# A hybrid RWKV-7 and forgetting-attention block: attention's logits tied to bulk steps, merge's first half in other banks, two gates moved

## The chip, the cores and the metric

The kernel is one program on one core of a Trainium2 chip. Its time is the device time in microseconds of one execution. TensorE (PE) does the matmuls and transposes, VectorE (DVE) and ScalarE (ACT) the elementwise work, GpSimd (POOL) some of it, and SyncE (SP) issues most DMAs. Each engine works through its own list of instructions in order. The order of these lists is fixed when the program is built.

## The reference

One block on x of 1024 tokens by 1024 channels, float32:

- h = rmsnorm(x) and u = h @ w_in, with 6,280 columns: for RWKV (r, k, v, two low-rank inputs, a gate), for attention (q, k, v, a gate, forget logits), and two gates g_a, g_b of 1,024 columns each.
- RWKV-7, 8 heads of 64: a token shift, then a scan over the tokens with a 64 x 64 state for each head, a norm for each head, a bonus term, times silu(gate).
- Forgetting attention, 8 heads of 64: q and k normed, logits q k / 8 plus the difference of cumulated log forget gates, causal softmax, times v, times silu(gate).
- merged = sigmoid(g_a) * (y_a @ w_out_a) + sigmoid(g_b) * (y_b @ w_out_b); then x + merged @ w_out and a last rmsnorm.

## The kernel before

Every projection is done in split precision: operands are kept as a high and a low part (`wH`, `wL`, `hTH`, `hTL`), and each k of the contraction takes three matmuls: high by high, high by low, low by high. The helper `laid` (L313) notes the third of them, so the list `laid_` has one entry for each such step, in the order in which the code emits them. A gate has 16 steps with 512 columns, a projection of v (two pairs of heads at once) 64 with 264 or 256, a projection of q and k for one pair 64 with 256.

The stages:

1. x is normed and transposed into `hTH` and `hTL`; the low-rank inputs and r, k, v of RWKV are projected.
2. RWKV runs in four units (pair of channel blocks p, half of the sequence n), here called units 0 to 3 = (0,0), (0,1), (1,0), (1,1). `prep` builds a unit's chunk matrices. Its matmuls `psc` (L587) come in two groups, and the second (e = 1) is the list `late_sc`. Behind it come masks on DVE, products on POOL, a bounce through DRAM and a triangular inverse by elimination on DVE (L663, L667), another bounce, transposes on DVE into `TW` (L679), and the small matmuls `pw` (L687) and `pz` (L698). Then `chain` walks through the unit's eight chunks, a serial chain of small matmuls and DVE and ACT work; `norm_out` ends the unit.
3. Attention runs over four pairs of heads. `project_qk` and `norm_qk` make q and k of a pair; `norm_qk` copies part of q to other partitions by DMA (QA<-QA, L988). `attend` goes over 8 blocks, four groups i of 256 queries by two heads h, with 2(i+1) parts of work in each: logits `sc` (L1024), a DVE pass (L1031), exp on ACT, transposes `pt`, products with V into `po`.
4. `merge` computes y_a @ w_out_a (`side` with key a: 16 tiles `pma`, 64 steps of 512 columns) and then y_b @ w_out_b (`pmb`). Its input `ya` takes the place of `hTL`, `m` that of `hTH`, and `yb` lies where attention's pool `fpa` lay, which holds V first of all. `parts` loads a piece of y through one of four ring slots and splits it on ACT (L1090) and DVE (L1091). The ring is used in fixed order; the pieces of `yb` are loaded between the columns c = 2 to 5 of the first half. Each `pma` tile is emptied by one DVE operation (L1124) with a gate piece `g`, loaded from `gab` through the same ring (L1118).
5. The last projection with w_out, the norm and the store.

What sets the order: every instruction has a priority, its place in the code. `order(LATER)` and `bulky()` put work far back, `order(-LATER)` far ahead. A planner walks a simulated time, and on each engine takes the instruction with the best priority whose operands are ready; this gives the fixed lists. Attention and `chain` are far ahead, and the "bulk" (gates, projections, merge) fills what they leave. The 24 gates are handed out by `fill`: RFILL[i] in the bulk of RWKV unit i; FPRE[p] before and FFILL[p] behind the projections of the next pair's q and k in `bulk_fox(p)`. Attention's pair 1 also has V of pairs 2 and 3 at the end of its bulk.

`not_before` adds an edge of program order without a semaphore: the named instructions come behind the given entry of `laid_` in PE's list. Before, it holds back `pw` of each unit, by PLACE; the call for `late_sc` is there but finds no name.

Bulk tiles go round PSUM banks by `bulk_tags`: RTAGS in RWKV, FTAGS (pj, pj, aux: three banks) in attention, TTAGS (seven) from merge on.

Of the kernel before, what the change touches and what calls it, by code (L numbers as in the profile page):

```python
# [53 lines left out]
PLACE = {  # L54
    "pw0_0": 179, "pw0_1": 294, "pw1_0": 398, "pw1_1": 502,
}
PACE = 0.3
# [19 lines left out]
RFILL = [5, 5, 3, 3]  # L77
FPRE = [1, 0, 0, 2]
FFILL = [1, 2, 2, 0]
# [15 lines left out]
def kernel(  # L95
# [215 lines left out]
    laid_ = []  # L311

    def laid(ins):  # L313
        laid_.append(ins.ins)

    def not_before(first, name):

        if name not in PLACE:
            return
        for ins in first:  # L320
            tc.add_manual_dep(
                ins, laid_[PLACE[name]].name,
                mybir.DependencyInfo(mybir.DependencyClass.NoSync, mybir.DependencyReason.DATA),
                reason="not_before",
            )
# [508 lines left out]
    def project_v(cb):  # L834
# [25 lines left out]
        for b in range(8):  # L860
# [3 lines left out]
            for k in range(KD):  # L864
                wH, wL = parts[k // KH]
                kk = k % KH
                nc.tensor.matmul(o, hTH[:, k, bs], wH[:, kk, :], start=(k == 0), stop=False)
                nc.tensor.matmul(o, hTH[:, k, bs], wL[:, kk, :], start=False, stop=False)
                laid(nc.tensor.matmul(o, hTL[:, k, bs], wH[:, kk, :], start=False, stop=(k == KD - 1)))
# [40 lines left out]
    def project_qk(p):  # L910
# [17 lines left out]
        for n in range(2):  # L928
            xt = fpa[0].tile([P, 4, QB], F32, tag="xn", name=f"xn{p}_{n}", bufs=2)
            rs = fpa[0].tile([P, 3, 16], F32, tag="rs", name=f"rs{p}_{n}", bufs=2)  # L930
            for b in range(4):
                bs = slice((4 * n + b) * P, (4 * n + b + 1) * P)
                ps = ps_pj(f"pf{p}_{n}_{b}")[:, :QB]
                for k in range(KD):
                    wH, wL = parts_[k // KH]
                    kk = k % KH
                    nc.tensor.matmul(ps, hTH[:, k, bs], wH[:, kk, :], start=(k == 0), stop=False)  # L937
                    nc.tensor.matmul(ps, hTH[:, k, bs], wL[:, kk, :], start=False, stop=False)  # L938
                    laid(nc.tensor.matmul(ps, hTL[:, k, bs], wH[:, kk, :], start=False, stop=(k == KD - 1)))  # L939
# [52 lines left out]
    sc_tags = SCTAGS  # L992

    def attend(p, KA, QA, qlo, cb):
        for i in range(4):
# [10 lines left out]
            for h, q in ((0, A), (1, B)):  # L1006
# [3 lines left out]
                for e in range(2):  # L1010
# [6 lines left out]
                    for g in range(ng):  # L1017
# [6 lines left out]
                        nc.tensor.matmul(sc[:, :mw], QA[:, h, qs], KA[:, h, ms], start=True, stop=False)  # L1024
# [74 lines left out]
    def merge():  # L1099
# [9 lines left out]
        with tc.tile_pool(name="yp", bufs=1, side="right", reuse_waits="tile") as yp:  # L1109
# [27 lines left out]
            for c in range(KD):  # L1137
                side(w_out_a, ya, 0, "a", c, then_a)
                if YB <= c < YB + 4:
                    for n in range(2):  # L1140
                        parts(c + 4 - YB, n, yb[:, 0], yb[:, 1])
            for c in range(KD):
# [52 lines left out]
    for p in range(4):  # L1195
        if not ATTFIRST:
            nxt = bulk_fox(p, None)
        with order(-LATER):
# [7 lines left out]
    bulk_tags[:] = TTAGS  # L1206
# [67 lines left out]
```

## Time and profile before

| | us |
|---|---|
| median of 3 runs (lowest to highest) | 1134.89 (1133.62 to 1138.43) |
| the profiled execution | 1135.76 |
| its span, first to last instruction | 1133.9 |
| mean granted clock of TensorE | 0.968 |
| DVE busy | 709.2 (63%) |
| ACT busy | 459.9 (41%) |
| POOL busy | 317.0 (28%) |

The span is cut into stages by what PE does: before 110 the input, the low-rank part and the first projections; RWKV's units up to about 597; attention's pairs, with borders at about 672, 748 and 860; merge from 944 to 1036; then the last projection. Times in the rows are microseconds from the span's start. A busy share counts an engine's records; matmuls overlap in them, so the pace of PE is read from the number of matmuls in a stretch. PEclk is the clock granted to TensorE, as a share of 2.4 GHz; it has the two levels 1.00 and 0.50. A value in brackets behind an instruction is the idle time of its engine before it and what ended that.

### The profile page before, as it was taken

To read this page: it belongs to the slowest core of one execution; us is meant where nothing else is said; L and a number is where in the kernel's file an instruction comes from. 1 tells how busy PE (TensorE), PEld (TensorE's weight loads), DVE (VectorE), ACT (ScalarE), POOL (GpSimd) and SP (SyncE) were. 2 spreads that over 40 slices of the span, in tenths; PEclk is the share of its full clock that TensorE was granted. 3 is DMA by queue.
4 is the path that set the end of the run, shared out by engine and by line. 5 is a ranking of instruction groups with operands and counts; after the bars stand their busy time and mean duration, and the time that the engine had idled before them with its cause. 6 is when DMAs were issued, how large, how long until landed. Compare 5 with 4: busy or idle time off the path is not lost. (4 is left out here: it accounts for less than half of the span.)

```text
span 1133.9 us, 18405 instructions
## 1 busy us (share of the span) xinstructions
PE 1052.9 (93%) x6591; PEld 871.7 (77%) x6591; DVE 709.2 (63%) x1855; ACT 459.9 (41%) x969; POOL 317.0 (28%) x467
## 2 busy tenths in 40 slices
PE   4989999999899999997998989979997999999997
PEld 3867777777677777777887877968896887887885
DVE  7414776699648883796678858652736823475145
ACT  6534323534243314431546636443544623223122
POOL 4420522252213421231113223222132222244400
PEclk9999999999989899998999989989998999999999
DMA  6256444144422433222024213232223126645133
GB/s 214 59 172 216 123 103 121 40 119 134 113 74 76 127 103 99 62 82 66 20 77 125 85 49 83 85 88 80 92 59 89 55 77 188 217 134 178 64 102 121
DMA packets 126684, 118.21 MB, mean 104 GB/s; under 512 B 33489, under 2 KB 91970, under 8 KB 126594
## 3 DMA queue, kind: packets, MB, share of 16 engines
q1 hardware_dynamic: 114304, 94.99, 29.1%
q10 hardware_dynamic: 11714, 21.52, 5.1%
q8 instruction: 52, 0.85, 0.3%
q0 software_dynamic: 576, 0.54, 0.2%
q14 instruction: 38, 0.31, 0.1%
HBM read 79.23 MB, written 35.68 MB: 101 GB/s over the span
## 5 line engine op out<-in xcount | busy, mean ns | idle before, releaser
L331 PE MATMUL ps_gg<-hTH,wH_gg 128*128 128x512 f32 x384 | 160.0, 417 | 0.8 <-DVE ql L982 0.6
L332 PE MATMUL ps_gg<-hTL,wH_gg 128*128 128x512 f32 x384 | 160.2, 417 | 0.0
L333 PE MATMUL ps_gg<-hTH,wL_gg 128*128 128x512 f32 x384 | 159.1, 414 | 0.0
L210 POOL TENSOR_TENSOR wL_gg<-w_gg,wH_gg 128x256 fp32r<-128x256 f32 x96 | 71.3, 774 | 194.2 <-ACT wH_gg L207 192.6
L331 PEld LDWEIGHTS ps_gg<-hTH,wH_gg 128*128 128x128 f32 x384 | 74.8, 195 | 15.5 <-issue 2.0
L333 PEld LDWEIGHTS ps_gg<-hTH,wL_gg 128*128 128x128 f32 x384 | 74.5, 194 | 13.9
L332 PEld LDWEIGHTS ps_gg<-hTL,wH_gg 128*128 128x128 f32 x384 | 74.6, 194 | 13.5
L938 PE MATMUL pf<-wqkL,hTH 128*128 128x256 f32 x256 | 73.7, 288 | 0.0
L939 PE MATMUL pf<-wqkH,hTL 128*128 128x256 f32 x256 | 73.7, 288 | 0.0
L937 PE MATMUL pf<-wqkH,hTH 128*128 128x256 f32 x256 | 73.5, 287 | 0.0
L396 ACT ACTIVATE gt<-ps_gg 128x512 f32<-128x512 f32 x40 | 23.9, 597 | 86.3 <-PE ps_gg L333 75.9
L1035 ACT ACTIVATE pr<-pr,mm 128x128 f32<-128x128 f32 (+3 forms) x64 | 49.9, 779 | 21.7 <-DVE mm L1031 19.4
L736 ACT ACTIVATE xw<-state,WC 64x64 f32<-64x64 f32 x112 | 38.7, 346 | 44.5 <-DVE state L756 37.3
L667 DVE TENSOR_TENSOR lt<-lt,etmp 64x30 f32<-64x30 f32 (+14 forms) x120 | 52.2, 435 | 3.7
L1228 PE MATMUL pz<-wo,mH 128*128 128x512 f32 (+1 forms) x136 | 52.4, 385 | 0.8 <-POOL wo L1097 0.8
L663 DVE TENSOR_TENSOR etmp<-lt 64x30 f32<-64x30 f32 (+14 forms) x120 | 47.7, 397 | 7.5 <-issue 4.0
L1227 PE MATMUL pz<-wo,mH 128*128 128x512 f32 (+1 forms) x136 | 51.8, 381 | 0.0
L1229 PE MATMUL pz<-wo,mL 128*128 128x512 f32 (+1 forms) x136 | 51.6, 379 | 0.0
L937 PEld LDWEIGHTS pf<-wqkH,hTH 128*128 128x128 f32 x256 | 49.2, 192 | 0.0
L938 PEld LDWEIGHTS pf<-wqkL,hTH 128*128 128x128 f32 x256 | 49.1, 192 | 0.0
L939 PEld LDWEIGHTS pf<-wqkH,hTL 128*128 128x128 f32 x256 | 49.0, 191 | 0.1
L1024 PE MATMUL sc<-KA,QA 128*128 128x384 f32 (+4 forms) x96 | 36.7, 390 | 12.0 <-DMA QA<-QA 11.9
(332 smaller groups left out, 2832.5 us busy)
## 6 DMA issues: line engine op xcount, KB each, us to landing
w_gg<-in_w_in_dram SPq DMA_DIRECT2D x24, 512.0 KB, 3.8
gab<-gt ACTq DMA_DIRECT2D x48, 256.0 KB, 2.0
ring<-gab SPq DMA_DIRECT2D x32, 256.0 KB, 3.1
xt<-in_x_dram SPq DMA_DIRECT2D x8, 512.0 KB, 6.1
wqk<-in_w_in_dram SPq DMA_DIRECT2D x16, 256.0 KB, 2.9
cb<-cumd SPq DMA_DIRECT2D x8, 512.0 KB, 4.1
ring<-yab SPq DMA_DIRECT2D x16, 256.0 KB, 3.7
ring<-in_w_out_dram SPq DMA_DIRECT2D x16, 256.0 KB, 3.1
```

The lines of the kernel that those rows point to most:

```text
L210: nc.gpsimd.tensor_sub(wL[:, k], w[:, k], wH[:, k])
L331: nc.tensor.matmul(ps, wH[:, k, :], rH[:, k, ts_], start=(k == 0), stop=False)
L332: nc.tensor.matmul(ps, wH[:, k, :], rL[:, k, ts_], start=False, stop=False)
L333: laid(nc.tensor.matmul(ps, wL[:, k, :], rH[:, k, ts_], start=False, stop=(k == nk - 1)))
L667: nc.vector.tensor_add(lt3[:, :s, s + 1 :], lt3[:, :s, s + 1 :], tm)
L937: nc.tensor.matmul(ps, hTH[:, k, bs], wH[:, kk, :], start=(k == 0), stop=False)
L938: nc.tensor.matmul(ps, hTH[:, k, bs], wL[:, kk, :], start=False, stop=False)
L939: laid(nc.tensor.matmul(ps, hTL[:, k, bs], wH[:, kk, :], start=False, stop=(k == KD - 1)))
L1035: nc.scalar.activation(pr[:, :w], pr[:, :w], AF.Exp, bias=last, scale=-1.0, accum_out=mm[:, 2:3])
L1227: nc.tensor.matmul(ps, mH[:, k, bs], oH[:, k, c], start=(k == 0), stop=False)
L1228: nc.tensor.matmul(ps, mH[:, k, bs], oL[:, k, c], start=False, stop=False)
L1229: nc.tensor.matmul(ps, mL[:, k, bs], oH[:, k, c], start=False, stop=(k == KD - 1))
```

## The change

- The planner's places for `pw` move, and `late_sc` of units 2 and 3 (names sc1_0 and sc1_1) gets places of its own.
- `laid` also keeps each step's number of columns. The new function `spread` takes, for each pair, the steps emitted from the pair's start (`since[p]`) to the next one's, for the last pair to the end of merge's first half, and puts the first logits of each of the 8 blocks behind the step at which the pair's columns have reached the block's share: 0, 5, 10, 20, 30, 45, 60 and 80%. Pair 0's first block stays free.
- The switch to TTAGS moves from before merge to behind its first half, so that half's 16 tiles use the three banks of attention's bulk.
- RFILL gives units 2 and 3 four gates each instead of three; FFILL takes both from pair 1.

```diff
@@ -52,8 +52,9 @@
 QKFIRST = True
 LATER = 1000000
 PLACE = {
-    "pw0_0": 179, "pw0_1": 294, "pw1_0": 398, "pw1_1": 502,
+    "pw0_0": 180, "pw0_1": 300, "sc1_0": 352, "pw1_0": 409, "sc1_1": 457, "pw1_1": 514,
 }
+SPREAD = 1.0
 PACE = 0.3
 PHPOOL = True
 APACE = 0
@@ -74,9 +75,9 @@
 NQEARLY = True
 ATTFIRST = True
 T1B = 3
-RFILL = [5, 5, 3, 3]
+RFILL = [5, 5, 4, 4]
 FPRE = [1, 0, 0, 2]
-FFILL = [1, 2, 2, 0]
+FFILL = [1, 0, 2, 0]
 
 
 def rsqrt_newton(nc, y, x, t):
@@ -308,18 +309,20 @@
     transposed(1, range(KD))
     xctx.close()
 
-    laid_ = []
-
-    def laid(ins):
+    laid_, cols_ = [], []
+
+    def laid(ins, cols=HALF):
         laid_.append(ins.ins)
+        cols_.append(cols)
 
     def not_before(first, name):
 
-        if name not in PLACE:
+        place = PLACE.get(name) if isinstance(name, str) else name
+        if place is None:
             return
         for ins in first:
             tc.add_manual_dep(
-                ins, laid_[PLACE[name]].name,
+                ins, laid_[place].name,
                 mybir.DependencyInfo(mybir.DependencyClass.NoSync, mybir.DependencyReason.DATA),
                 reason="not_before",
             )
@@ -866,7 +869,7 @@
                 kk = k % KH
                 nc.tensor.matmul(o, hTH[:, k, bs], wH[:, kk, :], start=(k == 0), stop=False)
                 nc.tensor.matmul(o, hTH[:, k, bs], wL[:, kk, :], start=False, stop=False)
-                laid(nc.tensor.matmul(o, hTL[:, k, bs], wH[:, kk, :], start=False, stop=(k == KD - 1)))
+                laid(nc.tensor.matmul(o, hTL[:, k, bs], wH[:, kk, :], start=False, stop=(k == KD - 1)), QB)
             pvv = pv[:, 0:256].rearrange("p (g h i) -> p g h i", g=2, h=2)
             for g, V in enumerate(vs_):
                 e = nc.scalar.copy(V[:, b, :, 0:HD], pvv[:, g])
@@ -936,7 +939,7 @@
                     kk = k % KH
                     nc.tensor.matmul(ps, hTH[:, k, bs], wH[:, kk, :], start=(k == 0), stop=False)
                     nc.tensor.matmul(ps, hTH[:, k, bs], wL[:, kk, :], start=False, stop=False)
-                    laid(nc.tensor.matmul(ps, hTL[:, k, bs], wH[:, kk, :], start=False, stop=(k == KD - 1)))
+                    laid(nc.tensor.matmul(ps, hTL[:, k, bs], wH[:, kk, :], start=False, stop=(k == KD - 1)), QB)
                 nc.scalar.copy(xt[:, b], ps)
                 sq = fpa[0].tile([P, QB], F32, tag="sq", name=f"sq{p}_{n}_{b}", bufs=2)
                 e = nc.scalar.activation(sq, ps, AF.Square)
@@ -990,6 +993,22 @@
         return KA, QA, qlo, cb
 
     sc_tags = SCTAGS
+    blocks = [[[] for _ in range(8)] for _ in range(4)]
+    since = []
+
+    def spread():
+
+        for p in range(4):
+            lo, hi = since[p], since[p + 1]
+            total = sum(cols_[lo:hi])
+            for k, first in enumerate(blocks[p]):
+                i, h = divmod(k, 2)
+                at, j = SPREAD * total * (i * (i + 1) + h * (i + 1)) / 20, lo
+                while at > cols_[j]:
+                    at -= cols_[j]
+                    j += 1
+                if k or p:
+                    not_before(first, j)
 
     def attend(p, KA, QA, qlo, cb):
         for i in range(4):
@@ -1021,7 +1040,9 @@
                         sc_tags.append(sc_tags.pop(0))
                         ks, ms = slice(g * gw, g * gw + gw), slice(g * gw, g * gw + mw)
                         end = g + 1 == ng
-                        nc.tensor.matmul(sc[:, :mw], QA[:, h, qs], KA[:, h, ms], start=True, stop=False)
+                        blocks[p][2 * i + h].append(
+                            nc.tensor.matmul(sc[:, :mw], QA[:, h, qs], KA[:, h, ms], start=True, stop=False).ins
+                        )
                         nc.tensor.matmul(
                             sc[:, :mw], QZ[:, h, e * P : (e + 1) * P], KA[:, h, ms], start=False, stop=not end
                         )
@@ -1139,6 +1160,9 @@
                 if YB <= c < YB + 4:
                     for n in range(2):
                         parts(c + 4 - YB, n, yb[:, 0], yb[:, 1])
+            since.append(len(laid_))
+            spread()
+            bulk_tags[:] = TTAGS
             for c in range(KD):
                 side(w_out_b, yb, 4, "b", c, then_b)
                 wo_part(wo[0], 0, c, ring())
@@ -1195,6 +1219,7 @@
     for p in range(4):
         if not ATTFIRST:
             nxt = bulk_fox(p, None)
+        since.append(len(laid_))
         with order(-LATER):
             attend(p, *qk)
         if ATTFIRST:
@@ -1203,7 +1228,6 @@
         if p == 0 and not ATTFIRST:
             with order(LATER):
                 project_v(1)
-    bulk_tags[:] = TTAGS
     tc.cur_priority += LATER
     mH, mL, wos = merge()
     zp = ctx.enter_context(tc.tile_pool(name="zp", bufs=1, side="right", reuse_waits="tile"))
```

## Rows read from the trace of the kernel before

**Rows 1.** The page, part 1: engine, busy us, share of the span, instructions.

```profile
PE 1052.9 (93%) x6591; PEld 871.7 (77%) x6591; DVE 709.2 (63%) x1855; ACT 459.9 (41%) x969; POOL 317.0 (28%) x467
```

**Rows 2.** Windows: us, busy (count) of PE, PEld, DVE, ACT, POOL; PEclk, DMA, GB/s.

```profile
304.00:536.00 232.00, 215.14 (x1568) 173.96 (x1568) 166.93 (x407) 80.99 (x176) 62.60 (x83) 0.94 0.31 88
307.40:317.60 10.20, 7.82 (x82) 5.74 (x77) 1.38 (x2) 4.44 (x7) 2.78 (x4) 0.50 0.44 143
372.30:382.50 10.20, 10.20 (x40) 8.52 (x40) 6.92 (x15) 2.76 (x5) 4.62 (x6) 0.50 0.42 125
525.90:532.70 6.80, 4.87 (x22) 4.90 (x23) 3.42 (x17) 0.00 (x0) 0.00 (x0) 0.50 0.30 57
664.00:682.00 18.00, 12.43 (x69) 10.30 (x68) 10.93 (x26) 8.67 (x15) 3.19 (x5) 0.81 0.27 71
...
682.00:740.00 58.00, 56.91 (x409) 50.55 (x408) 42.27 (x133) 32.27 (x83) 16.80 (x37) 1.00 0.27 79
...
852.00:874.00 22.00, 14.57 (x82) 12.55 (x80) 12.78 (x35) 9.87 (x20) 6.02 (x10) 0.77 0.33 86
860.40:870.60 10.20, 6.49 (x20) 5.37 (x21) 7.07 (x13) 3.59 (x5) 3.32 (x6) 0.50 0.39 103
```

**Rows 3.** Windows: ten microseconds of nothing but gate projections.

```profile
925.00:935.00 10.00, 10.00 (x45) 8.04 (x44) 0.00 (x0) 2.13 (x3) 1.64 (x3) 1.00 0.30 105
```

**Rows 4.** Timeline of PE: start, duration, work, count, [idle before, releaser].

```profile
748.24 0.77 PE L1024 MATMUL sc<-KA,QA 128*128 128x256 f32 x2 [3.96 <-DMA QA<-QA]
752.48 1.11 PE L971 MATMUL pqk<-ident,xn 128*128 128x128 f32 x4 [3.47 <-DVE xn L967]
...
604.72 0.66 PE L971 MATMUL pqk<-ident,xn 128*128 128x128 f32 x2 [2.13 <-DVE xn L967]
```

**Rows 5.** Windows from the start, of L333 (gates, k, r, v), then of L869 (V).

```profile
0.00:370.90 370.90, 139.51 (x343) 65.39 (x343) 0.98 0.41 121
...
0.00:485.50 485.50, 180.61 (x443) 84.57 (x443) 0.98 0.39 115
...
0.00:535.60 535.60, 11.93 (x39) 8.36 (x39) 0.97 0.38 111
```

**Rows 6.** Timeline of PE, then of DVE: late psc, pw and V.

```profile
370.94 2.54 PE L587 MATMUL psc<-AR,BK 64*128 64x128 f32 x16 [1.39 <-DVE BK L578]
...
425.00 0.24 PE L687 MATMUL pw<-TW,Tb 32*32 32x32 f32 x2
...
485.59 2.02 PE L587 MATMUL psc<-AR,BK 64*128 64x128 f32 x16
...
527.83 0.56 PE L867 MATMUL pfv<-wvH,hTH 128*128 128x264 f32 x1 [7.12 <-DVE lf L878]
...
535.64 1.20 PE L687 MATMUL pw<-TW,Tb 32*32 32x32 f32 x64
...
427.25 0.44 DVE L679 STREAM_TRANSPOSE TW<-Tb 32x256 f32<-32x256 f32 x1 [0.65 <-DMA Tb<-td]
...
534.43 0.43 DVE L679 STREAM_TRANSPOSE TW<-Tb 32x256 f32<-32x256 f32 x1
```

**Rows 7.** Window of the gate tiles alone; then timelines: last block, ya, yb, m.

```profile
865.00:944.00 79.00, 54.80 (x192) 36.33 (x192) 0.00 (x0) 4.33 (x8) 0.96 0.27 84
...
902.37 0.48 PE L1024 MATMUL sc<-KA,QA 128*128 128x512 f32 x1
...
916.42 0.28 PE L1069 MATMUL po<-PHL,V 128*128 128x256 f32 x1
...
943.33 0.62 ACT L1090 CAST ya<-ring 128x512 fp32r<-128x512 f32 x1 [4.77 <-PE ps_gg L332]
...
961.70 1.25 ACT L1090 CAST yb<-ring 128x512 fp32r<-128x512 f32 x2 [4.29 <-DMA ring<-yab]
...
979.76 0.62 ACT L1090 CAST yb<-ring 128x512 fp32r<-128x512 f32 x1 [1.71 <-DMA ring<-yab]
...
954.52 0.69 DVE L1124 SCALAR_TENSOR_TENSOR m<-ring,pma 128x512 f32<-128x512 f32 x1 [2.46 <-DMA ring<-gab]
```

## The prediction

> **What bounds the kernel now.** First the page's engine table: PE is busy for 1052.9 of 1133.9 us [rows 1]. No other engine comes near, and the change neither adds nor drops an instruction, so time can leave only where PE stands idle or runs at its lower clock. To find those places I read the windows by stage [rows 2]; the reader is to compare PE's busy time with the length of the window, and to look at PEclk.
>
> - RWKV units 1 to 3 (304 to 536): 232.0 - 215.1 = 16.9 us idle. Inside lie three stretches at 0.50 of the clock (1.2 GHz), after PE had stood idle or worked in small pieces, with PE busy for 7.82, 10.20 and 4.87 us. Work at half clock takes twice its time, so half of that busy time is lost: 11.4 us. Together 28.3 us.
> - The three borders between attention's pairs, of which the first and the last stand in the rows: 5.6, 7.4 and 7.4 us idle (the middle one is as the last). Each has a stretch at half clock; in the last one 6.49 us of it are busy, and I take 6 for each, so 9.0 us are lost. Together 29.4 us.
> - Between two borders (682 to 740): 56.91 of 58.0 us busy at clock 1.00. Here nothing is to be had.
>
> So 57.7 us is all that the change can reach. Then PE's timeline at a border [rows 4]: the pair's first logits wait 3.96 us for the copy QA<-QA, and behind them the transposes of the second half wait 3.47 us for xn. PE is strictly in order: gate matmuls that need neither are queued behind both.
>
> **The change part by part.** I count bulk work in steps (three matmuls over one k, what `laid` records). A gate's step takes 0.70 us: 45 matmuls touch a window of 10 us, so about 43 fit, 0.233 us each [rows 3]. V's matmuls have 264 columns for 512, so 0.12 each and 0.36 a step; a step of q and k, with 256 columns, I take as equal.
>
> *Ties of the logits.* For pairs 1 to 3 the first block now comes behind the first step of the pair's own bulk, and the last at 80% of it. The copy QA<-QA that it needs is issued in the middle of the pair before: behind the projections of q and k come one gate in pair 0 (16 steps, 11.2 us), V in pair 1 (64 steps, 23 us) and two gates in pair 2 (22.4 us), and blocks of attention besides. Each is over the 3.96 us, so the wait goes at all three borders. What is late next is xn: transposes of the second half wait for DVE's chain behind the last projection. The nearest row is pair 0's own, where fill is at hand: 2.13 us [rows 4]. I keep that three times, 6.4 us, and 0.6 for a clock that falls at one of them: 7 stay, of 29.4, a gain of 22.5 (rounded up). Bounds: nothing stays (29.4), or each border keeps 3.47 with its half clock of 3.2 (20 stay, gain 9.5). The ties themselves are program order without a semaphore. What they hold back is attention's own chain. Its matmuls take some 31 us a pair (the last pair's 79 us from 865 on, nearly without idle, less 192 gate matmuls of 0.233 and 2.8 lost to half clock [rows 7]); with two gates, and q and k, a pair has 77 us. The last and longest block has a fifth of that, 15.4, and takes 14.3 [rows 7]. I cost the ties at nothing, under cover of the bulk steps; without cover each would show the 3 to 4 us of its first waits.
>
> *Places in RWKV and two gates.* The late `psc` of unit 2 now comes after step 352 instead of 343, and the chain ahead of it ends 6 steps later (300 for 294), so it lies 4 steps, 2.8 us, later in its own terms [rows 5]: over its wait of 1.39 [rows 6]. With that wait I let the half clock right behind it go (5.1 us). `pw` of unit 1, whose waits led into the first half clock, moves 6 steps, 4.2 us, and off the gate evacuation that held ACT. For `pw` of units 2 and 3 the question is when TW is there.
>
> - Unit 2: TW is ready 427.7 - 370.9 = 56.8 us after the late `psc` [rows 6]; at full clock `psc` gives back some 2.5 of it (its first 16 matmuls took 2.54 us against 2.02 in unit 3, the other 16 lay wholly in the half clock). PE had 56 steps up to `pw` (343 to 399) and now has 57 (353 to 410): 425.0 - 370.9 = 54.1 us less 5.1 of half clock plus 0.7 is 49.7. Wait 54.3 - 49.7 = 4.6; if all that leads to TW were as short as in unit 3 (49.3), none. I take 3.
> - Unit 3: TW is ready 534.9 - 485.6 = 49.3 us after. Between lay 21 gate steps and 39 of V [rows 5], 14.7 + 14.0 = 28.7 of 50.05 us; with 7.1 idle at V and 2.4 lost, 11.8 are other work and small waits. Now they are 38 and 19: 26.6 + 6.8 + 11.8 = 45.2. Wait 4.1, and more if the small waits go: the 7.12 us stop at V (it waits for DVE, which is in the elimination [rows 6]) turns into a smaller one at `pw`. Take 5.
>
> 8 us of waits, and 4 us for clock that falls with them (the three stretches above cost 2.4 to 5.1): 12 stay of 28.3, gain 16. Bounds: all goes (28.3); or both waits are as long as the 7.12 us at V, with the dearest half clock each (5.1): 24 stay, gain 4. The gates bring 96 matmuls, which leave pair 1 as they enter here, and their DMAs, one load of 512 KB and two stores each: SP and ACT issue the same number as before. They have no DVE work, and that is why they fit beside the elimination. If this cover were gone, 22.4 us would come on top.
>
> *Merge's first half.* 64 steps, 45 us, that may now run beside the last pair. PE's work is the same. ya's casts still wait for the last gate's matmul as the 943.33 row shows [rows 7]: a new tile waits for the whole old one. Along go 8 casts of 0.62 us on ACT, 24 DVE operations of 0.69, and on SP 8 loads of yab, 16 of gab and four of weights, now queued between the pair's QZ and yg loads and its yab stores, which wait for POOL. DVE has room: 42.3 of 58.0 busy beside a full PE [rows 2].
>
> The cost lies behind it. The last block starts at 80%, 19 steps before merge's first half ends: 13.4 us of bulk, plus a fifth of attention's 31 and a rest of the block before, 7.5, so PE has 21 us of work. The block itself takes 916.7 - 902.4 = 14.3 us [rows 7]. yb lies where V lay, so I let its casts wait for the last read of V. Then four rounds through two ring slots: from the first cast to the last DVE half 979.76 + 0.62 + 0.69 - 961.70 = 19.4 us [rows 7]. I take 15 to 19, as part of that was other traffic. Second half ready at 14.3 + 15 to 19 = 29 to 34, PE free at 21: 8 to 13 idle, less 2 that it can start on yb's first parts, plus 2 for half clock. I take 10, bounds 0 (yb waits only for its own region) and 22 (the worst of these and a 5 us gab load behind the last round). Before, 27 us of gates and all of merge's first half covered this.
>
> *Banks.* Those 16 tiles go round three banks instead of seven. The first DVE operation that empties one waited 2.46 us for its gab load and came 10.6 us after ya's first cast [rows 7]. Three banks hold 8.4 us of PE work, and with attention between, 12. I take 0.
>
> The three-bank window shows clock 1.00 [rows 2]. Against this stands a rule of the Trainium skill ("TensorE: Matmul & The Clock Gate", "A second HAM failure mode: psum-queue depth-cycling"): going round the PSUM banks can leave micro-idles that make the clock swing between its two levels. By the row the banks cost nothing; by the rule the sum would rise by what the rival below works out.
>
> **Sum.** -22.5 - 16 + 10 = -28.5 us against the profiled execution (1135.8: the span of 1133.9 and 1.9 around it; 0.9 over the median of the runs): **1107 us**.
>
> **The rivals.**
>
> - *The waits in RWKV move instead of going.* Unit 2's and 3's chains take 50 to 57 us whatever PE does, as the two sums above show; for it, PE comes earlier than TW in both. Against it, 11.0 us more work lies in the stretch (26 gate steps more, 20 of V fewer). Gain 4 instead of 16: 1119.
> - *No hole behind the last pair* (yb does not wait for V, or the last block ends early): 1097. Against it, the 943.33 row.
> - *The ties bind nothing at the borders*: the scheduler starts a pair's bulk before the copy has landed, and the logits behind the first step wait as now. For it, a tie to one step is short (0.4 us); against it, everything in the former pair's bulk ranks ahead. Gain 16 - 10 = 6 alone: 1130.
> - *Slower: the clock falls beside the last pair.* PE is in order, the logits are tied to bulk steps, and each step needs one of three banks, emptied only when its gab load has landed. A late load stops bulk and attention alike, and PE goes on in small pieces, as from 372 on, where the clock was low with PE fully busy (10.20 of 10.20) after 1.39 us idle. Merge's first half is 192 matmuls of 0.233 = 44.7 us; at half clock it takes 44.7 more: 1152. It decides from 28.5 us on, with nearly two thirds of that work at 1.2 GHz. For it, the gab wait of 2.46 and attention's 128-column pieces; against it, clock 1.00 in the same mixture on the same three banks (682 to 740). The Trainium skill's rule above, from its TensorE page, describes this case; no row here bears it out.
>
> **How the numbers follow.** Forecast 0.52, waits move 0.15, no hole 0.10, ties bind nothing 0.10, clock 0.13. About 0.5% (5.7 us) is what a measurement can tell from no change: faster is under 1129, slower over 1141. The first three are faster, and 0.03 of the fourth: 0.80; the rest of the fourth 0.07; slower 0.13. The bounds added up give 1135.8 - 28.3 - 29.4 = 1078 and 1135.8 - 4 - 9.5 + 22 = 1144. From 1085 to 1131 lies about 0.8.
>
> **What would show it.** No wait of sc for QA at the borders, clock 1.00 from one pair into the next, and pq waits of 1 to 3 us. `psc` of unit 2 without a wait; V without its 7.12; `pw` of units 2 and 3 with 2 to 6. Merge's first matmuls among the last pair's attention, and a hole of some 8 us before the second half's, ended by yb. It is wrong if attention's matmuls wait at many blocks (operands later than the ties), if PE idles inside a pair for more than 3 us, or if the hole is over 20.

## The result and the profile after

The changed kernel is slower: 1162.84 us (median of 4 runs, 1159.72 to 1162.99) against 1135.99 for the kernel before in the same comparison, ratio 1.023, 95% interval 1.020 to 1.026. The prediction was 1107 us with a range of 1085 to 1131, so it was wrong in sign. The profiled execution took 1162.99, its span is 1161.3, the mean granted clock 0.961 (before 0.968). In the rows of every changed kernel, line numbers are 3 higher than before up to `spread`, and up to 24 higher behind it.

The page's engine line after; it answers to [rows 1]:

```profile
PE 1069.3 (92%) x6591; PEld 876.6 (75%) x6591; DVE 716.8 (62%) x1855; ACT 459.7 (40%) x969; POOL 316.7 (27%) x467
```

PE has the same 6591 matmuls, yet is busy 16.4 us longer, and idle 92.0 us of the span (1161.3 - 1069.3) where it was 81.0. So the loss has two halves, and idle time is the smaller one. The windows after, stage by stage and then at the three borders, in merge's first half, its second half and the start of the last projection (columns: us; busy and count of PE, PEld, DVE, ACT, POOL; PEclk, DMA share, GB/s), answer to [rows 2]:

```profile
260.00:304.00 44.00, 37.59 (x217) 29.12 (x216) 39.21 (x92) 13.22 (x23) 15.36 (x18) 1.00 0.41 117
304.00:400.00 96.00, 91.79 (x695) 72.97 (x694) 60.27 (x145) 37.93 (x80) 30.42 (x39) 0.98 0.37 105
400.00:500.00 100.00, 98.98 (x670) 78.64 (x668) 72.70 (x179) 34.10 (x74) 30.25 (x37) 1.00 0.29 84
500.00:627.00 127.00, 112.06 (x882) 100.83 (x883) 72.82 (x211) 43.55 (x108) 25.95 (x36) 0.87 0.24 68
690.00:706.00 16.00, 9.74 (x38) 7.71 (x36) 10.39 (x23) 7.83 (x13) 3.22 (x5) 0.68 0.36 91
760.00:778.00 18.00, 11.93 (x68) 10.50 (x67) 13.28 (x30) 10.44 (x19) 6.64 (x11) 0.72 0.28 81
855.00:870.00 15.00, 9.14 (x37) 7.12 (x36) 10.28 (x25) 8.34 (x14) 6.52 (x11) 0.66 0.37 97
935.00:1007.00 72.00, 68.48 (x335) 52.57 (x335) 42.73 (x89) 27.89 (x55) 15.38 (x26) 0.98 0.39 126
1007.00:1055.00 48.00, 46.14 (x195) 35.99 (x194) 32.71 (x45) 15.62 (x25) 15.78 (x14) 1.00 0.45 143
1058.00:1071.00 13.00, 8.42 (x23) 5.69 (x22) 6.63 (x9) 5.45 (x10) 6.55 (x5) 0.74 0.66 222
```

Units 2 and 3 are better filled up to 500 (98.98 of 100 us busy), and from 500 on worse than before. The borders are hardly better: 6.3, 6.1 and 5.9 us idle, each with a clock near 0.7. Counted as in the prediction, idle time and half of the busy time at 1.2 GHz, they lose 28.6 us where it was 29.4. New losses stand at 260 to 304 and at the last projection. Added up over both traces, idle time plus half of the time that PE was busy at 1.2 GHz:

| stretch (before / after) | before | after | difference |
|---|---|---|---|
| start to 260 | 25.5 | 26.2 | +0.7 |
| to pair 0's norm (597 / 627) | 36.8 | 42.7 | +5.9 |
| attention and merge's first half (to 986.5 / 1007) | 36.6 | 39.9 | +3.3 |
| merge's second half and last projection | 9.2 | 17.8 | +8.6 |
| PE's own time, as if all at full clock | 1025.7 | 1034.6 | +8.9 |

The differences add up to 27.4, by which the span grew. Half is a round count: in the rows below a gate matmul starts every 0.43 us at 1.2 GHz (697.21 and 697.64), and at 2.4 GHz every 0.233 [rows 3], so it takes 1.8 times as long, not twice. PE's timeline after has the waits behind these numbers (start, duration, work, [idle before, releaser]); they answer to [rows 4, 6, 7]:

```profile
274.00 0.47 PE L334 MATMUL ps_gg<-hTH,wH_gg 128*128 128x512 f32 x1 [1.47 <-DVE last_gg L367]
...
383.17 1.01 PE L590 MATMUL psc<-AR,BK 64*128 64x128 f32 x7 [1.94 <-DVE Q L596]
...
542.56 0.31 PE L690 MATMUL pw<-TW,Tb 32*32 32x32 f32 x2 [5.18 <-DVE TW L682]
...
595.56 0.55 PE L940 MATMUL pf<-wqkH,hTH 128*128 128x256 f32 x1 [2.54 <-DVE lf L905]
...
618.72 0.55 PE L974 MATMUL pqk<-ident,xn 128*128 128x128 f32 x3 [3.57 <-POOL xn L970]
...
686.81 0.60 PE L1069 MATMUL pt<-ident,pr 128*128 128x128 f32 x4
687.17 0.36 PE L941 MATMUL pf<-wqkL,hTH 128*128 128x256 f32 x1
687.37 0.28 PE L942 MATMUL pf<-wqkH,hTL 128*128 128x256 f32 x1
687.49 0.28 PE L940 MATMUL pf<-wqkH,hTH 128*128 128x256 f32 x1
...
696.65 0.76 PE L334 MATMUL ps_gg<-hTH,wH_gg 128*128 128x512 f32 x1 [5.14 <-DVE ql L985]
697.21 0.63 PE L335 MATMUL ps_gg<-hTL,wH_gg 128*128 128x512 f32 x1
697.64 0.63 PE L336 MATMUL ps_gg<-hTH,wL_gg 128*128 128x512 f32 x1
...
771.99 1.12 PE L974 MATMUL pqk<-ident,xn 128*128 128x128 f32 x4 [3.64 <-DVE xn L970]
...
864.62 0.90 PE L974 MATMUL pqk<-ident,xn 128*128 128x128 f32 x3 [3.64 <-DVE xn L970]
...
953.77 0.44 PE L1044 MATMUL sc<-KA,QA 128*128 128x384 f32 x1 [1.98 <-DVE mm L1052]
...
1010.87 0.49 PE L334 MATMUL pmb<-yb,wH_ob 128*128 128x512 f32 x1 [1.38 <-ACT yb L1111]
...
1064.04 0.74 PE L1251 MATMUL pz<-wo,mH 128*128 128x512 f32 x1 [3.40 <-ACT wo L1117]
1065.60 0.79 PE L1252 MATMUL pz<-wo,mH 128*128 128x512 f32 x1 [0.82 <-POOL wo L1118]
```

No logits wait for QA any more. But a gate waits 5.14 us for `ql` at the first border, and the transposes wait 3.64 for xn at the others. Pair 0's first transposes, which did not wait before, now wait 3.57 us for the xn that POOL makes. The four rows from 686.81 on show a switch from transposes to a projection. Behind the projection's first matmul (0.36 long) the next starts 0.20 later, and the one after that 0.12 later. But the first itself starts only 0.03 behind the last transpose (at 687.14 in the trace), so the two steps together take 0.23 us, as two steps without a switch do (0.11 and 0.12). This switch cost nothing.

### The profile page after: what moved, and what is told of

Its sections match the earlier page's. It is cut to its first block, busy times and chain, and to the rows that moved or that the text cites. A ratio compares the mean times of both kernels' runs of the same rounds, so it can differ in the third digit from the quotient of the medians.

```text
span 1161.3 us, 18377 instructions
## 1 busy us (share of the span) xinstructions
PE 1069.3 (92%) x6591; PEld 876.6 (75%) x6591; DVE 716.8 (62%) x1855; ACT 459.7 (40%) x969; POOL 316.7 (27%) x467
## 5 line engine op out<-in xcount | busy, mean ns | idle before, releaser
L335 PE MATMUL ps_gg<-hTL,wH_gg 128*128 128x512 f32 x384 | 157.5, 410 | 0.0
L336 PE MATMUL ps_gg<-hTH,wL_gg 128*128 128x512 f32 x384 | 156.4, 407 | 0.0
L211 POOL TENSOR_TENSOR wL_gg<-w_gg,wH_gg 128x256 fp32r<-128x256 f32 x96 | 76.0, 821 | 173.6 <-ACT wH_gg L208 147.0
L334 PEld LDWEIGHTS ps_gg<-hTH,wH_gg 128*128 128x128 f32 x384 | 73.6, 192 | 29.4 <-issue 9.3
L1089 PE MATMUL po<-PHL,V 128*128 128x256 f32 x160 | 47.9, 312 | 5.4 <-ACT PHL L1079 2.5
L1069 PE MATMUL pt<-ident,pr 128*128 128x128 f32 x288 | 48.4, 278 | 3.3 <-DVE pr L1060 1.3
```

What stands on the lines that cost most here:

```text
L211: nc.gpsimd.tensor_sub(wL[:, k], w[:, k], wH[:, k])
L334: nc.tensor.matmul(ps, wH[:, k, :], rH[:, k, ts_], start=(k == 0), stop=False)
L335: nc.tensor.matmul(ps, wH[:, k, :], rL[:, k, ts_], start=False, stop=False)
L336: laid(nc.tensor.matmul(ps, wL[:, k, :], rH[:, k, ts_], start=False, stop=(k == nk - 1)))
```

## Experiments

All ratios are to the kernel before, run beside on the same chip; unless said otherwise an experiment is the kernel before with the edit shown. Four runs first took the change apart.

**The RWKV part alone** (places and two gates).

```diff
-    "pw0_0": 179, "pw0_1": 294, "pw1_0": 398, "pw1_1": 502,
+    "pw0_0": 180, "pw0_1": 300, "sc1_0": 352, "pw1_0": 409, "sc1_1": 457, "pw1_1": 514,
-RFILL = [5, 5, 3, 3]
+RFILL = [5, 5, 4, 4]
-FFILL = [1, 2, 2, 0]
+FFILL = [1, 0, 2, 0]
```

> The kernel before with the new places of pw and late psc and the two moved gates, without ties and with merge's banks as before. Theory A (the changed kernel's trace read stage by stage: from 260 us to pair 0's norm_qk it lost 42.6 us to idle time and half clock where before lost 36.8): about 6 slower, 1142 (1138 to 1148), with gate matmuls of unit 1 waiting 1.2 to 1.9 us for DVE five times near 274 to 314, pw of unit 3 waiting about 5 and half clock at 582 to 600. Rival B (the RWKV part gains as predicted, and it is the ties that spoil it by drawing other work forward): 1120 to 1128, without the five gate waits.

1142.38 us, ratio 1.004 (1.001 to 1.007): theory A, and with its signs: gate waits of 1.2 to 2.1 from 273 to 314, `pw` of unit 3 waiting 5.00, the last chain's waits from 584 on.

**Ties for pairs 0 to 2 alone.**

```diff
+                if p < 3 and (k or p):
+                    not_before(first, j)
```

> The kernel before with ties for the logits of pairs 0, 1 and 2 alone; places, gates and banks as before. Theory A (the wait for QA goes, but PE stands just as long for xn and ql of norm_qk, which sits in the same three banks as the bulk behind it; and some 60 more switches between bulk and attention cost 0.08 us each): 1136 to 1146, likeliest 1140, with 3 to 5 us of waits for xn or ql at the borders. Rival C (the borders of the changed kernel were long only because pair 1 had lost its two gates as cover; with them back the ties pay): 1114 to 1125, waits of at most 2 us at the first two borders.

1143.23, ratio 1.006 (1.004 to 1.009). The border waits are those of the changed kernel (5.15 for `ql`, 3.33 and 3.64 for xn), though pair 1 had its two gates. Rival C falls.

**Ties for pair 3 alone, with the later switch of banks.**

```diff
+                if p == 3:
+                    not_before(first, j)
```

> The kernel before with ties for the last pair alone, over its gates and merge's first half, and the later switch of banks. Theory A (the last block comes late, so yb's pieces hold the ring's slots when w_out's pieces should load, and the last projection waits for them with a fall of the clock: 8.7 us in the changed kernel, and some 25 switches more): 1144 to 1150. Rival D (the lateness of w_out's pieces comes from the whole schedule's shift, not from the tie of the last pair): 1134 to 1140, the last projection without a wait over 1 us.

1147.0, ratio 1.010 (1.007 to 1.012). The three parts cost 0.4, 0.6 and 1.0%, together 2.0 of the 2.3% lost: all parts lose, none rescues another.

**Ties for first blocks alone.**

```diff
+                if not k and p:
+                    not_before(first, j)
```

> The kernel before with a tie for the first block of pairs 1 to 3 alone (behind the first step of the pair's own bulk); everything else as before. Theory A (the wait for QA turns into a wait for xn behind the projections, no new switches): 1133 to 1140. Rival E (the first block's tie is what pays, and the ties of the later blocks cost): 1114 to 1126, with the half clock at the borders gone.

1140.7, ratio 1.004 (1.001 to 1.006): theory A, 0.7 us above its range. This is the clearest picture of what was misjudged. At its second border PE has one wait:

```profile
756.60 1.09 PE L974 MATMUL pqk<-ident,xn 128*128 128x128 f32 x4 [8.29 <-DVE xn L970]
```

DVE's timeline of the same stretch:

```profile
748.17 0.42 DVE L948 TENSOR_REDUCE rs<-sq 128x4 f32<-128x256 f32 x1 [2.41 <-ACT sq L945]
...
749.25 0.17 DVE L90 TENSOR_TENSOR rs<-rs 128x16 f32<-128x16 f32 x1
749.46 0.68 DVE L983 TENSOR_TENSOR KA<-pqk,KA 64x512 fp32r<-64x512 f32 x1
...
751.97 0.55 DVE L90 TENSOR_TENSOR rs<-rs 128x16 f32<-128x16 f32 x1
752.55 0.76 DVE L985 SCALAR_TENSOR_TENSOR ql<-pqq,gqk,QA 64x512 fp32r<-64x512 f32 x1
...
753.34 0.55 DVE L91 SCALAR_TENSOR_TENSOR rs<-rs 128x16 f32<-128x16 f32 x1
753.93 0.65 DVE L92 SCALAR_TENSOR_TENSOR rs<-rs 128x16 f32<-128x16 f32 x1
754.61 0.17 DVE L90 TENSOR_TENSOR rs<-rs 128x16 f32<-128x16 f32 x1
...
755.23 1.22 DVE L970 TENSOR_TENSOR xn<-xn,rs 128x1024 f32<-128x1024 f32 x1
```

And POOL's:

```profile
751.77 2.77 POOL L211 TENSOR_TENSOR wL_gg<-w_gg,wH_gg 128x256 fp32r<-128x256 f32 x4 [10.43 <-ACT wH_gg L208]
```

The wait for QA is gone and the one for xn has grown to 8.29 us, which is the old border in one piece: 3.96 for QA, 0.77 of logits, 3.47 for xn make 8.20 [rows 4]. From 748.17 to 756.45 DVE walks through the norm of the second half, with the first half's KA and `ql` in between, and PE stands for all of it. QA's wait had only been the first to show.

The next four runs asked why nothing covers that chain, and took the RWKV part further apart.

**Norm of the first half emitted between the two projections.**

```diff
         for n in range(2):
             ... project half n of q and k ...
+            if p:
+                norm_half(p, n, xn, rr, done)
```

> The kernel before, where the norm of the first half of q and k for pairs 1 to 3 is emitted between the two halves' projections instead of behind both; no ties, places and gates as before. Theory A (a border is DVE's chain behind the last projection: 0.42 reduce, nine operations of 0.2, 1.2 for xn, and in between 2.9 of work for the first half's KA and ql; the first-half work and the QA copy now lie under the second half's projections): the wait for QA goes and the one for xn falls to 4 us or less, half clock mostly gone; 1116 to 1128. Rival F (the length of that chain doesn't matter, as bulk that could cover is held by other things): waits of the same sum, 1133 to 1140.

1152.46, ratio 1.011 (1.007 to 1.016): slower, and a miss of theory A. At the second and third border pqk still waited 6.67 and 3.05, and the first half's transposes got waits of their own between the two projections (5.76 at 861). The step was no remedy: it made two chains of one, and neither was covered. In the 6.67 us DVE works on the second half alone, from the reduce at 758.64 to the end of xn at 764.64, without any of attention's work between; in the 5.76 us DVE and then POOL work on the first half, and PE, which has just ended its projection, stands.

**First-block ties, pqk and pqq of pairs 1 to 3 in the misc banks** (the edit on top of the run before last).

```diff
-  pq = ps_misc(f"pq{key}{p}_{n}", PQTAG[c]) if p == 0 else ps_pj(f"pq{key}{p}_{n}")
+  pq = ps_misc(f"pq{key}{p}_{n}", PQTAG[c] if p == 0 else "misc")
```

> As the run with ties for first blocks alone, but pqk and pqq of pairs 1 to 3 take the misc banks of the logits instead of the three banks of the bulk. Theory G (bulk behind norm_qk can't cover the wait, because its tiles come next in the three banks that pqk and pqq hold until ql is done): the 8.29 us waits fall to 4 or less and the time to 1120 to 1132. Rival H (PE's order puts pqk of the second half ahead of that bulk whatever the bank): 8 us waits stay, 1137 to 1143.

1127.7, ratio 0.990 (0.985 to 0.994), where the same ties without the bank edit gave 1.004. Theory G. PE at its second border:

```profile
750.23 0.40 PE L336 MATMUL ps_gg<-hTH,wL_gg 128*128 128x512 f32 x1
752.67 0.63 PE L974 MATMUL pqk<-ident,xn 128*128 128x128 f32 x4 [2.05 <-DVE xn L970]
753.14 0.60 PE L974 MATMUL pqq<-ident,xn 128*128 128x128 f32 x4
753.50 0.48 PE L334 MATMUL ps_gg<-hTH,wH_gg 128*128 128x512 f32 x1
```

DVE's chain is as long as before (744.17 to 752.52 in that trace), but gate matmuls now run up to 750.6 while it works, and 2.05 us of the wait are left at all three borders. This agrees with the rule of the Trainium skill ("Perfetto Trace Analysis", section "Matmuls") that independent matmul groups should go round different PSUM banks, so that emptying one overlaps the next group.

**New places for `pw` of units 0 and 1 alone.**

```diff
-    "pw0_0": 179, "pw0_1": 294, "pw1_0": 398, "pw1_1": 502,
+    "pw0_0": 180, "pw0_1": 300, "pw1_0": 398, "pw1_1": 502,
```

> The kernel before with the new places of pw for units 0 and 1 alone (180 and 300). Theory A2 (holding pw of unit 1 back by 6 more steps leaves PE nothing but gates whose banks DVE empties late, in the elimination): the five gate waits of 1.2 to 2.0 between 270 and 316 come back, the half clock at 307 goes; net 1136 to 1140. Rival I (the waits come from the moved gates and the late psc): no waits there, 1130 to 1135.

1137.09, ratio 0.998 (0.995 to 1.001). The five gate waits are there (1.52, 1.30, 1.38, 1.24 and 1.04 from 271.77 to 311.25), and the waits and half clock of `pw` at 306 are gone: theory A2, and a wash. In this trace `pw` of unit 2 also waits 2.15 and 1.00 for 1.42 and 0.39, with 10.2 us of half clock from 428.7; the run with first-block ties and other banks has such a stretch at 424.6 without the move. Each gate wait is ended by the DVE operation that empties the bank. In the first four DVE is in the elimination; ahead of the fifth it has itself waited 5.00 us for ACT. That the six more steps before `pw` make the gates wait is argued, not shown: the first wait comes more than 40 us ahead of `pw` of unit 1 (314.95), and `pw` of unit 0 moved too.

**Units 2 and 3 alone: the two gates (RFILL and FFILL as in the first run), late psc, their pw.**

```diff
-    "pw0_0": 179, "pw0_1": 294, "pw1_0": 398, "pw1_1": 502,
+    "pw0_0": 179, "pw0_1": 294, "sc1_0": 352, "pw1_0": 409, "sc1_1": 457, "pw1_1": 514,
```

> The kernel before with the two moved gates and the new places for units 2 and 3 (late psc and pw), but pw of units 0 and 1 where they were. Theory A2 (the gates fill units 2 and 3, but V is then used up before the last chain, so PE idles and runs at half clock at 582 to 600, some 12 us given back): 1136 to 1142. Rival I (units 2 and 3 gain as predicted once unit 1 is left alone): 1124 to 1131.

1140.87, ratio 1.001 (0.999 to 1.004): theory A2. PE's waits for `pw` of unit 3 and in the last chain:

```profile
543.78 0.31 PE L690 MATMUL pw<-TW,Tb 32*32 32x32 f32 x2 [5.30 <-DVE TW L682]
...
583.06 1.03 PE L727 MATMUL px<-state,AR 128*128 128x128 f32 x4 [0.79 <-ACT wqkH L208]
584.88 0.63 PE L742 MATMUL pu<-xw,Tb 128*128 128x64 f32 x4 [0.79 <-DVE xw L732]
...
588.42 1.33 PE L727 MATMUL px<-state,AR 128*128 128x128 f32 x4 [0.85 <-DVE state L759]
...
596.07 0.55 PE L940 MATMUL pf<-wqkH,hTH 128*128 128x256 f32 x1 [2.54 <-DVE lf L905]
```

The window from 500 on (columns as above):

```profile
500.00:630.00 130.00, 114.06 (x892) 102.54 (x892) 73.07 (x211) 45.15 (x112) 25.60 (x36) 0.87 0.24 68
```

V's last step lies ahead of the row at 583; from there the chain's small matmuls stand alone, and by the 0.87 a quarter of the window is at 1.2 GHz. The next bulk, q and k of pair 0, starts at 596.07 only, released by DVE's `lf`. In the kernel before it runs from 561.7 on, beside the chain.

Four more tested the two explanations in place.

**The whole change, with pqk and pqq in the misc banks** (the bank edit above).

> The changed kernel whole, but pqk and pqq of pairs 1 to 3 take the misc banks instead of the bulk's. Theory G (the borders of the changed kernel stand because the bulk that should cover them comes next in banks that pqk and pqq hold): the border waits of 5.14, 3.64 and 3.64 fall to about 2 and the time by 8 to 14 us against the changed kernel, to 1149 to 1155; what is left of the loss (RWKV 5, switches, the last projection) stays, so it remains slower than before. Rival J (with logits tied block by block the misc banks are in use at the borders and pq waits for those instead): 1158 to 1165.

1143.67, ratio 1.005 (1.002 to 1.008) where the change alone had 1.023. One line takes back 1.8% of the time, more than theory G asked; no wait for xn or `ql` is left at the borders behind pair 0's. What remains over 1.000 is as expected: `pw` 5.09, and the last projection waiting 3.23 and 1.24 for w_out. Attention's own matmuls wait up to 2.02 us for DVE behind the first border.

**Pair 3's ties with shares times 0.6.**

```diff
-SPREAD = 1.0
+SPREAD = 0.6
```

> As the run with ties for pair 3 alone, but the blocks' shares times 0.6, so that the last block starts at 48% of the columns instead of 80%. Theory A (the last block's late end holds the ring's slots and delays w_out's pieces): no wait over 1 us in the last projection and none at merge's second half; 1138 to 1142, about 6 less than that run. Rival D (the last projection's wait comes from elsewhere): 1144 to 1148 with a wait of 1.5 or more.

1138.43, ratio 1.001 (0.999 to 1.004) where full shares gave 1.010: theory A. The last projection's longest wait falls to 0.74; with full shares that run had

```profile
1047.77 0.50 PE L1251 MATMUL pz<-wo,mH 128*128 128x512 f32 x1 [1.85 <-ACT wo L1117]
1049.13 0.61 PE L1252 MATMUL pz<-wo,mH 128*128 128x512 f32 x1 [0.86 <-POOL wo L1118]
```

**Other banks without any tie.**

> The kernel before with pqk and pqq of pairs 1 to 3 in the misc banks, without any tie. Theory G (the bank is what matters; but without a tie the pair's first logits still stand ahead in PE's order and wait 3.96 for QA): half the gain of the run with both, 1130 to 1135. Rival K (ties add nothing once the banks are free): 1124 to 1129. Rival L (logits ahead wait for QA and hold PE through the whole chain as before): 1136 to 1140.

1117.99, ratio 0.984 (0.981 to 0.987): better than any theory said. Logits of the next pair don't wait for QA here either: they use the same misc banks as pqk and pqq, and PE's list has them behind these. So the ties were not needed at the borders. From 640 to 944, first-block ties, then other banks with those ties, then other banks alone:

```profile
640.00:944.00 304.00, 277.06 (x1830) 245.20 (x1829) 177.20 (x518) 141.74 (x338) 76.07 (x149) 0.96 0.26 76
```

```profile
640.00:944.00 304.00, 292.24 (x1908) 256.38 (x1907) 184.55 (x531) 149.99 (x350) 80.24 (x154) 0.99 0.30 88
```

```profile
640.00:944.00 304.00, 294.21 (x1913) 256.11 (x1914) 184.91 (x530) 150.38 (x348) 79.73 (x155) 0.99 0.30 91
```

With other banks PE does some 80 matmuls more in the same 304 us, and PEclk goes from 0.96 to 0.99. Of the 6.2 us between the spans of the last two kernels, 5.6 are more half clock in RWKV, which no tie touches, so whether first-block ties still cost something is left open.

**First-block ties, other banks, and late psc of unit 2.**

```diff
-    "pw0_0": 179, "pw0_1": 294, "pw1_0": 398, "pw1_1": 502,
+    "pw0_0": 179, "pw0_1": 294, "sc1_0": 348, "pw1_0": 401, "pw1_1": 502,
```

> As the run with first-block ties and other banks, and in addition late psc of unit 2 behind step 348 and its pw behind step 401 (398 before), no other place or gate changed. Theory M (the wait of 1.39 at late psc and the half clock behind it go, and nothing starves later, as no bulk is moved): 4 to 7 less than that run, 1120 to 1124. Rival N (the wait moves on to pw of unit 2): 1126 to 1130.

1121.87, ratio 0.987 (0.985 to 0.989), against 0.990 (0.985 to 0.994) without: not told apart. Theory M's condition wasn't met: late psc waits 1.63 us in its second 16 matmuls instead of 1.39 in front of the first, and the half clock behind it lasts 6.8 us instead of 10.2. V now waits 10.49 instead of 7.11.

Then three for the part in RWKV that was still open, and for a better kernel.

**Units 2 and 3, with a fifth gate in unit 3.**

```diff
-RFILL = [5, 5, 4, 4]
+RFILL = [5, 5, 4, 5]
-FPRE = [1, 0, 0, 2]
+FPRE = [1, 0, 0, 1]
```

> As the run with units 2 and 3 alone, but unit 3 has five gates instead of four (one of the last pair's gates moves there); places the same, so 16 more steps of V are left behind pw of unit 3. Theory A2 (the last chain stood idle and at half clock at 582 to 600 because V was used up ahead of pw): the five waits of 0.8 to 2.5 there shrink to two or fewer and the time falls to 1131 to 1136. Rival O (the planner draws the extra work forward and the end of the chain starves as before): 1137 to 1142 with waits of the same sum.

1130.97, ratio 0.994 (0.992 to 0.996) where four gates gave 1.001. The five waits of the last chain are gone and `pw` waits 1.78 for 5.30, but new ones stand at `pz` and behind the chain:

```profile
550.69 0.31 PE L701 MATMUL pz<-Tb,TW 32*32 32x32 f32 x2 [3.52 <-ACT TW L695]
...
599.08 0.66 PE L899 MATMUL pcs<-lf,tri 128*128 128x64 f32 x2 [5.39 <-DVE stat L91]
```

From 500 on the clock is 0.92 for 0.87:

```profile
500.00:630.00 130.00, 116.71 (x928) 104.08 (x926) 72.79 (x210) 45.82 (x112) 29.04 (x39) 0.92 0.27 75
```

**Other banks and late psc of unit 2, no ties.**

> As the run with other banks and no ties, and in addition late psc of unit 2 behind step 348 and its pw behind step 401. Theory M (that gain adds up): 2 to 5 less than that run, 1113 to 1116. Rival N (what is gained at late psc is lost at V, which waited 10.49 instead of 7.10 in the run with ties): 1117 to 1121.

1120.28, ratio 0.984 (0.980 to 0.988), as without (0.984). Rival N: V waits 10.48 us for 7.10, and psc still 1.63. What the shorter half clock behind psc gains (6.8 us for 10.2), V gives back.

**Other banks and five gates in unit 3, no ties.** The edits of the two runs together.

> The run with five gates in unit 3 (places and gates of units 2 and 3, no ties), with pqk and pqq of pairs 1 to 3 in the misc banks in addition. Theory A and G together (separate stretches of the program): the product of the two ratios, 0.994 times 0.984 = 0.977, 1109 to 1114. Rival P (the gate taken from the last pair was cover that the third border now lacks): 1115 to 1121, a border wait over 4.

1106.07 us, ratio 0.973 (0.969 to 0.978): faster than both kernels, and with the product of the two ratios (0.977) inside the interval: the two gains add up. No border waits over 2.06 us for xn, so rival P falls. Its page:

```profile
PE 1042.2 (94%) x6591; PEld 864.1 (78%) x6591; DVE 703.3 (64%) x1855; ACT 459.2 (42%) x969; POOL 318.8 (29%) x467
```

## Why the prediction was wrong

*What can be reached.* The 57.7 us of idle time and half clock were there, and the last kernel shows that some 30 can be had; as a matmul at 1.2 GHz takes 1.8 times as long and not twice, 57.7 is some 2 us too high. But "here nothing is to be had" between the borders was read as "nothing is to be lost" too.

*Ties of the logits: the step that failed.* That the QA wait goes at all three borders was right. "What is late next is xn", kept at 2.13 each, was the error. Of the 29.4 us at the borders I let 7 stay; 28.6 stayed. The 2.13 of pair 0 was taken as the nearest row because "fill is at hand" there; but pair 0's pqk and pqq have other banks than the bulk (PQTAG), and those of pairs 1 to 3 come from the bulk's three. A gate or V tile behind them takes a bank that `ql` has still to empty (the 5.14 for `ql` says so in the row), and PE's order puts the second half's transposes ahead. So the cover that I counted, one gate, V, two gates, wasn't usable. Measured: 8.29 with ties of the first blocks alone; 2.05 with other banks, close to the 2.13 that I had priced without its condition. The gain of 22.5 became a loss of about 0.6%; my lower bound, a gain of 9.5, rested on each border keeping only one of its two waits, and the two were one.

*Ties "at nothing".* This failed too. Attention's matmuls and the bulk took 589.0 us of PE's time for 579.9, counted as if at full clock: 4.0 us of the rise come in the run with ties for pairs 0 to 2, 1.5 with pair 3, and 1.8 with the RWKV part alone. Spreading raised the changes in PE's list between the two kinds from 312 to 395 (55 and 30 more in the two runs with ties), but that a change has a price isn't shown: other banks without ties bring 23 more changes and 0.1 us. A wait shorter than the overlap of two matmuls (a record of 0.28 us at a pace of 0.12) isn't recorded as idle, so many small waits would look the same; no run tells these apart. Recorded inside pairs are seven waits of 0.4 to 0.9 us and one of 1.98. None is over 3 us, but beside the last pair (870 to 1007) the idle time adds up to 3.7, over the sign that I had named.

*Places in RWKV and two gates.* V's 7.12 went, and `pw` of unit 3 waited 5.18 where I had taken 5. But late psc waits 1.94, now in its second 16 matmuls, and `pw` of unit 2 not at all, where I had 3. Two costs were missing: `pw` of unit 1 moved 6 steps later was counted as gain alone, while five gate waits (7.3 us) come with it; and V used before `pw` was missing beside the last chain, with half clock from 582 to 600. 26 more gate steps for 20 fewer of V were in the prediction, as work that fills; where V is missing I didn't look, nor at pair 0's first transposes, which now wait 3.57. The first rival, that waits move instead of going, is what happened, and it cost more than the rival's price, a gain of 4: 42.7 us lost there, 36.8 before.

*Merge's first half.* Its size came out near, by chance; its place did not. I expected 10 us ahead of the second half; there the trace has 1.6. The rest came later: the pieces of yb that follow the last block went into the ring from 1002.67 on, behind them the pieces of w_out came late, and the last projection waited 3.40, 0.82 and 0.35 and lost 3.0 to half clock. 9.2 us in all. The run with shorter shares takes it away but for 0.74, so the late last block is shown as the cause; that the ring is the way from one to the other is read from the order of the loads.

*Three banks, and the slower rival.* The 0 held: between 935 and 1007 no `pma` waits for a bank. The clock beside the last pair stayed at 1.00 but for 954.9 to 958.3, behind the 1.98 at 953.77. The result was slower, but not by that rival. The Trainium skill's rule that I had weighed ("TensorE: Matmul & The Clock Gate", "A second HAM failure mode: psum-queue depth-cycling") would make the clock swing where PE goes round the banks with frequent small idle gaps. In the stretch at 260 to 304 gates go round three banks with gaps of 1.2 to 1.5 us, some 7 us apart, and PEclk is 1.00: there the gaps cost their own length and no more. Whether more frequent gaps would do it isn't shown here.

## What to carry to other kernels

When a wait is to be taken away, find the longest chain that ends behind it, on any engine: at a strictly ordered engine two waits in a row can be one chain seen twice, and the second grows by what the first gives up. Before work is counted as cover, ask which buffers its tiles take next, and who still holds them; a price read from a similar place holds only if its buffers are the same. Bulk that fills a hole earlier is missing later, and matmuls spread more finely can take an engine longer although no wait is recorded.

## What the runs showed of the hardware

- At 1.2 GHz a gate matmul of 512 columns starts every 0.43 us (rows at 697.21 and 697.64), at 2.4 GHz every 0.233 [rows 3]: 1.8 times, for half the clock.
- With ties PE's own time rose by 4.0 and 1.5 us, though no wait is recorded for it. It does not follow the number of changes between kinds of matmul (55 and 30 more there, 23 more for 0.1 us with other banks), and at 687 a change cost nothing.
- In the DVE rows at the border above, operations on 16 elements take 0.55 to 0.65 us instead of 0.17, three times, all while POOL splits a weight (751.77 to 754.54), and the next one after takes 0.17 again. `ql`, which reads its first operand from PSUM, took its usual 0.76 in between. This agrees with the Trainium skill ("SBUF — State Buffer", "Who interferes with whom"): a DVE instruction with two SBUF inputs contends with a GpSimd instruction that reads SBUF. It adds 1.2 us to the chain that a border waits for; no run took POOL's work away to show what it is worth.
- Four gaps of 1.2 to 1.5 us in PE's work, about 7 us apart, left the granted clock at 1.00 from 260 to 304 in the changed kernel.
